# Fp32 hybrid decoder block: the third memory head's keys ahead of the fourth's, the first head's division two units later

## The chip, the cores and the metric

The kernel runs on one core of a Trainium2 chip. The core has five engines, each with its own instruction queue: TensorE (PE in the profile, with its weight loads as PEld), VectorE (DVE), ScalarE (ACT), GpSimd (POOL) and SyncE (SP), which here issues most transfers. Engines wait for each other through semaphores; each works through its own queue in order. The metric is the device time of one execution, in microseconds (us); the time of a kernel is the median of several executions.

## The reference

One decoder layer over 1024 tokens of width 1024, in float32. The parts that the change touches are the keys and values of the memory attention, and the forgetting attention.

```python
u = rms_norm(h, norm_mix[l])
proj = u @ w_in[l]
u_ssm, q, k, v, f_logit, gate_logits = jnp.split(proj, [...], axis=-1)
y_ssm = jax.nn.gelu(s5_ssm(u_ssm, ...))
att = forgetting_attention(q, k, v, f_logit + b_forget[l])   # 8 heads of width 64, causal
h = h + (gate_a * out_a + gate_b * out_b) @ w_mix_out[l]
h = h + memory_cross_attention(rms_norm(h, norm_mem_q[l]), rms_norm(mem, norm_mem_kv[l]), ...)
h = h + (jax.nn.silu(f_a) * f_b) @ w_ffn_out[l]
return rms_norm(h, norm_final)

# forgetting_attention, for one block of queries
s = einsum('bhqd,bhkd->bhqk', qb, kh) * scale + cb[..., :, None] - cum[..., None, :]
p = softmax(where(causal, s, -inf))
out = einsum('bhqk,bhkd->bhqd', p, vh)

# memory_cross_attention: 256 memory tokens, 4 heads of width 128
k, v = split(m @ w_kv, 2, axis=-1)
```

## The kernel before

Each float32 operand is held as a high part (a cast to fp32r on ACT, line 183) and a low part (the rest, a subtraction on DVE, line 184); the helper is `split`. A product is then three matmuls: high by high, low by high, high by low (lines 173 to 175).

The **input stage** (`stage_in`) does four things at once. It loads the two memory tiles and the eight token tiles, computes their norms (squares on ACT, roots on DVE and POOL, the scaling on line 231), transposes them on TensorE (line 237, in PSUM banks named `misc`, `pv` and `mm`) and splits the result into `mh`/`ml` (memory) or `uh`/`ul` (tokens). It splits the weights of the memory's keys and values and of the state-space input into `whi`/`wlo`. It computes the keys of four memory heads (`keys`, 8 steps of three 128x256 matmuls each, in `mm` banks), their values (sums named `sc`), and the first products of the state-space branch (`mm<-uh,whi`). What is written when is told by the string `ORDER_IN`, one word for each step: `K2` is the product for the third head's keys, `k2` its split, `W2` the split of its weight, `T20` and `T21` the transposes of token tile 2, `E20` and `E21` their split (`Em0`, `Em1`, `En0`, `En1` for the two memory tiles), `V` a quarter of the values, `U00` the first state-space product.

The order of this string is not yet the order on the engines. The framework's scheduler places the instructions: each engine takes first what by the scheduler's own estimates of durations is ready first, and the written order decides between them; `behind` adds an edge by hand. So a step that is moved in the string moves others with it.

The **forgetting attention** (`Fox.run`) goes through eight heads. For each it has 12 units: unit `i` computes the scores of one block of 128 keys against up to 512 queries (`scores`, lines 1793 and 1794 in banks `sc`), the exponential on ACT (line 1800), a high and a low part (`ph`, `pl`; in some units the cast is on DVE, line 1802, and the subtraction on POOL, line 1803), and the products with the values two units later (lines 1818 to 1825 in banks `pv`). Work of other heads is laid beside the units: the projection of the head after next (lines 173 to 175 into `mm`, read by ACT and DVE on lines 1725 to 1733), and the running maximum of the next head (`row_max`: line 1763 on TensorE into `mm`, lines 1765 and 1768 on DVE). There are three `mm` banks; projections hold them for long.

When a head is done, its sums `num` are copied out (line 1827), the denominators go through DRAM and come back as `rb`, and `divide` multiplies `num` by `rb` (line 1846), splits the result into `ahi` and `alo` (lines 183 and 184) and stores both. It is called in the next head, behind unit 5. There is one buffer for `num`, so the next head's copy on line 1827 waits until `alo` has been made.

Of the kernel before, what the change touches and what calls it, by code (L numbers as in the profile page):

```python
# [38 lines left out]
RSLOT_LATE = (0, 1, 2, 3, 4, 4, 5, 5, 6, 6, 7, 7)  # L39

ORDER_IN = """
Fm G0 Fn G1 D0 X10 B0 b0 Qm Qn Rm D1 Sm F1 B1 Tm0 Tm1 b1 Rn Sn Tn0 F0 D2 Em0 Tn1 En0 W0 Em1 En1 D3 F2 F3 W1 C1 Q0 Q1 K0 D4 F4 F5 K1 R0
S0 T00 T01 k0 E00 Q2 W2 D5 F6 F7 E01 S1 T10 Q3 W3 k1 K3 K2 W4 E10 W5 D6 R1 k2 T11 k3 S2 Q4 V0 S3 T30
E11 D7 D8 D9 Da Q5 T20 R2 T21 E21 E20 S4 E30 W6 Db y0 L0 W7 T40 V1 S5 E40 T31 V2 E31 W8 T41 V3 E41 W9 T50 Q6 v T51 E51
U00 Q7 R3 S6g u00 L1 T60 E50 S7g Wa T61 T70 E61 Wb U10 E60 T71 E70 E71 P0 y1 U20 u10 u20 P1 U21 U11 U30
P2 u30 U31 u11 u31 U01 u21 P3 P4 P5 u01
# [1531 lines left out]
class Fox:  # L1578
# [280 lines left out]
    def run(self, y_d, yT, aT, w_glu, w_d, filler):  # L1859
# [8 lines left out]
        def load_y(k, h):  # L1868

            with B.behind(self.maxima[NH - 2] if h else self.spread[NH - 4]):  # L1870
                for i, dst in enumerate(yT.rhs(k, h)):
                    S.dma_start(f32(dst).rearrange("p (t c) -> p t c", t=4),
                                y_d[k, i, 4 * h:4 * h + 4].rearrange("t p c -> p t c"))

        def first_glu(i, f):
            with B.behind(self.spread[3] if i < 9 else self.maxima[NH - 2]):
                f()

        def load_att(k):
            for h in range(2):  # L1880
                for i, dst in enumerate(aT.rhs(k, h)):
                    S.dma_start(f32(dst), self.att_d[i, k * P:(k + 1) * P, 512 * h:512 * h + 512])
# [31 lines left out]
        for h in range(NH):  # L1914
            side = {i: [] for i in range(12)}
            late = h == NH - 2
            if late:
                for i, f in enumerate(pro[h + 1].parts[8:]):
                    side[i // 2].append(f)
                side[3].append(pro[h + 1].evac[1])  # L1920
            if h + 1 < NH:
                for i, f in enumerate(self.row_max(h + 1)):
                    side[(RSLOT_LATE if late else RSLOT)[i]].append(f)
                side[9].append(lambda: self.max_row(h + 1))
            if h + 2 < NH:
                n = 8 if h + 3 == NH else 16
                for i, f in enumerate(pro[h + 2].parts[:n]):
                    side[i if n == 8 else PSLOT[i]].append(f)
                side[9].append(pro[h + 2].evac[0])
                if n == 16:  # L1930
                    side[11].append(pro[h + 2].evac[1])
            if h + 3 < NH:
                side[9].append(lambda: pro[h + 3].split(self.exp))
            for n_ in {1: (4, 5), 2: (6,), 3: (7,)}.get(h, ()):
                side[5].append(lambda n_=n_: pro[n_].load(self.spread[h - 1]))
            if h == 0:
                side[0].append(lambda: self.values_of_v(0, 7))
            if late:
                for k in range(8):
                    side[4 + k].append(lambda k=k: load_y(k % 4, k // 4))  # L1940
            if h == NH - 1:
                for k in range(3):
                    side[6 + k].append(lambda k=k: load_att(k))
                for i, f in enumerate(filler):
                    side[i * 12 // len(filler)].append(lambda i=i, f=f: first_glu(i, f))
            for i, u in enumerate(units):
                self.scores(h, *u)
                for f in side[i]:
                    f()
                if len(self.hi_todo) > 2:  # L1950
                    self.values_hi()
                if len(self.lo_todo) > 1:
                    self.values_lo()
                if h and i == 5:
                    with B.behind(self.left):
                        self.divide(h - 1)
        while self.hi_todo:
# [33 lines left out]
```

## Time and profile before

| | us |
|---|---|
| median of 3 runs | 1540.33 (1538.91 to 1540.62) |
| the profiled execution | 1539.77 |
| its span, first to last instruction | 1538.1 |

The profile is of one execution. Its timeline gives for each instruction the start and the duration in us, the engine, the line, what it writes and reads, and in brackets the idle time of the engine before it with what ended it. Matmuls are pipelined: on TensorE the distance between two starts, not the duration, is what one costs.

### The profile page before, as it was taken

What the parts mean: (1) busy time and instruction counts of PE and PEld (TensorE: products, weight loads), DVE (VectorE), ACT (ScalarE), POOL (GpSimd) and SP (SyncE); (2) the same over time, 40 slices, a digit from 0 to 9 for tenths busy, and PEclk for the clock granted to TensorE, in tenths of its full rate; (3) what the DMA queues carried; (4) which work ended last, traced back from release to release, by engine and by line L of the source; (5) the groups of instructions that cost most, each with busy time, mean ns of one, the idle gap of its engine ahead of it and who ended that gap; (6) DMA issues with size and microseconds to landing.
All of it is one profiled execution on the core that took longest, in us unless ns stands there. A gap on an engine that the chain in (4) does not pass through costs nothing. (4 is left out here: it accounts for less than half of the span.)

```text
span 1538.1 us, 20434 instructions
## 1 busy us (share of the span) xinstructions
PE 1520.7 (99%) x7329; PEld 1257.7 (82%) x7329; DVE 1005.7 (65%) x1828; ACT 658.1 (43%) x1183; POOL 253.6 (16%) x341
## 2 busy tenths in 40 slices
PE   8999999999999999999999999999999999999998
PEld 7888888898777678888888888888888888888886
DVE  7936554355878867675556797777777775675555
ACT  7423334324667643232435663333333333354343
POOL 1166542100121214100102200000000000101001
PEclk9999999999999999999999999999999999999999
DMA  9634556611223746378210356555544544896542
GB/s 286 161 104 102 131 128 144 180 41 16 50 46 88 192 131 198 111 218 308 89 69 1 117 204 210 162 161 160 158 158 157 157 145 139 291 391 220 192 163 110
DMA packets 196293, 234.06 MB, mean 152 GB/s; under 512 B 35576, under 2 KB 127656, under 8 KB 195680
## 3 DMA queue, kind: packets, MB, share of 16 engines
q1 hardware_dynamic: 188704, 214.93, 47.0%
q10 hardware_dynamic: 7488, 17.83, 3.1%
q8 instruction: 57, 0.93, 0.3%
q14 instruction: 44, 0.36, 0.1%
HBM read 161.94 MB, written 72.71 MB: 153 GB/s over the span
## 5 line engine op out<-in xcount | busy, mean ns | idle before, releaser
L184 DVE TENSOR_TENSOR wlo<-raw,whi 128x1024 fp32r<-128x1024 f32 (+2 forms) x120 | 126.3, 1058 | 45.4 <-ACT whi L183 44.2
L183 ACT CAST whi<-raw 128x1024 fp32r<-128x1024 f32 (+2 forms) x120 | 108.7, 910 | 105.6 <-PE mm L174 39.1
L184 DVE TENSOR_TENSOR ol<-or,oh 128x1024 fp32r<-128x1024 f32 x73 | 90.1, 1236 | 74.0 <-ACT oh L183 71.9
L173 PE MATMUL mm<-uh,whi 128*128 128x512 f32 x344 | 136.5, 397 | 0.0
L174 PE MATMUL mm<-ul,whi 128*128 128x512 f32 x344 | 135.1, 393 | 0.0
L175 PE MATMUL mm<-uh,wlo 128*128 128x512 f32 x344 | 134.5, 391 | 0.0
L183 ACT CAST oh<-or 128x1024 fp32r<-128x1024 f32 x73 | 76.9, 1054 | 105.0 <-PE mm L1108 34.2
L997 POOL TENSOR_TENSOR g<-a,c 128x512 f32<-128x512 f32 x22 | 35.7, 1621 | 389.0 <-ACT a L996 389.0
L175 PEld LDWEIGHTS mm<-uh,wlo 128*128 128x128 f32 x344 | 64.7, 188 | 13.3 <-DVE wlo L184 0.2
L1803 POOL TENSOR_TENSOR pl<-pf,ph 128x512 fp32r<-128x512 f32 (+1 forms) x32 | 36.8, 1152 | 232.5 <-DVE ph L1802 193.3
L173 PEld LDWEIGHTS mm<-uh,whi 128*128 128x128 f32 x344 | 64.8, 188 | 11.6
L174 PEld LDWEIGHTS mm<-ul,whi 128*128 128x128 f32 x344 | 64.8, 188 | 11.0
L1800 ACT ACTIVATE pf<-sc 128x512 f32<-128x512 f32 (+1 forms) x96 | 46.4, 489 | 44.5 <-DVE sc L1796 28.3
L986 DVE SCALAR_TENSOR_TENSOR c<-c,pv 128x512 f32<-128x512 f32 x22 | 15.1, 687 | 76.5 <-ACT c L985 76.4
L211 POOL TENSOR_TENSOR r<-ms,mhalf 128x1 f32<-128x1 f32 (+1 forms) x26 | 15.7, 605 | 298.6 <-DVE ms L207 258.5
L964 PE MATMUL pv<-S3h,we 128*128 128x512 f32 x176 | 57.7, 389 | 0.0
L1806 DVE TENSOR_TENSOR pl<-pf,ph 128x512 fp32r<-128x512 f32 (+2 forms) x64 | 35.3, 553 | 10.4 <-ACT ph L1805 9.8
L1108 PE MATMUL mm<-ol,oh 128*128 128x512 f32 (+1 forms) x110 | 41.9, 381 | 0.0
L1108 PE MATMUL mm<-oh,ol 128*128 128x512 f32 (+1 forms) x110 | 41.9, 381 | 0.0
L1108 PE MATMUL mm<-oh 128*128 128x512 f32 (+1 forms) x110 | 41.9, 381 | 0.0
L173 PE MATMUL sc<-uh,whi 128*128 128x512 f32 x104 | 40.8, 392 | 0.0
L173 PE MATMUL mm<-yh,whi 128*128 128x512 f32 x104 | 40.7, 392 | 0.0
(639 smaller groups left out, 4554.2 us busy)
## 6 DMA issues: line engine op xcount, KB each, us to landing
or<-c_d SPq DMA_DIRECT2D x77, 256.0 KB
wo<-in_w_ffn_out_dram SPq DMA_DIRECT2D x22, 512.0 KB
c_d<-g SPq DMA_DIRECT2D x44, 256.0 KB
t_d<-wo SPq DMA_DIRECT2D x44, 256.0 KB
or<-t_d SPq DMA_DIRECT2D x44, 256.0 KB
rawb<-in_w_ffn_in_dram SPq DMA_DIRECT2D x20, 512.0 KB
raw<-in_w_ffn_in_dram SPq DMA_DIRECT2D x20, 512.0 KB
raw<-in_w_in_dram SPq DMA_DIRECT2D x19, 512.0 KB
```

The source lines that it names most:

```text
L173: T.matmul(ps, lh, rh, start=first, stop=False)
L174: T.matmul(ps, lh, rl, start=False, stop=False)
L175: return T.matmul(ps, ll, rh, start=False, stop=last)
L183: cast = self.A.copy(hi, src)
L184: self.rest = (self.G if pool_lo else self.V).tensor_sub(lo, src, f32(hi))
L211: self.G.tensor_tensor(out=r, in0=v, in1=self.mhalf[:, 0:n], op=ALU.pow)
L964: T.matmul(ps, l_[:, k, :], r_, start=first and k == 0 and i == 0, stop=k == 3 and i == 2, skip_group_check=True)
L997: G.tensor_mul(g[:, 512:], a1, c1)
L1108: T.matmul(ps, l_[:, gi], r_[:, c0:c1], start=k == 0 and (p == NP - LAST if own else p == 0 and n in (1, 2, 7)), stop=p == NP - 1 and k == ...
L1800: self.exp = A.activation(pf[:, off:], ps[:, off:], AF.Exp)
L1803: G.tensor_sub(pl[:, off:], pf[:, off:], f32(ph[:, off:]))
L1806: self.left = V.tensor_sub(pl[:, off:], pf[:, off:], f32(ph[:, off:]))
```

## The change

In `ORDER_IN` the step `Em1` (the second half of a memory tile's cast and subtraction) is written ahead of the transposes `Tn1`, and `K2` ahead of `K3`. In the attention, `divide` is called behind unit 7 in the second head (`h == 1`, so for the first head's sums) and behind unit 5 in the others, as before. Nothing is added or taken away.

```diff
-Fm G0 Fn G1 D0 X10 B0 b0 Qm Qn Rm D1 Sm F1 B1 Tm0 Tm1 b1 Rn Sn Tn0 F0 D2 Em0 Tn1 En0 W0 Em1 En1 D3 F2 F3 W1 C1 Q0 Q1 K0 D4 F4 F5 K1 R0
-S0 T00 T01 k0 E00 Q2 W2 D5 F6 F7 E01 S1 T10 Q3 W3 k1 K3 K2 W4 E10 W5 D6 R1 k2 T11 k3 S2 Q4 V0 S3 T30
+Fm G0 Fn G1 D0 X10 B0 b0 Qm Qn Rm D1 Sm F1 B1 Tm0 Tm1 b1 Rn Sn Tn0 F0 D2 Em0 Em1 Tn1 En0 W0 En1 D3 F2 F3 W1 C1 Q0 Q1 K0 D4 F4 F5 K1 R0
+S0 T00 T01 k0 E00 Q2 W2 D5 F6 F7 E01 S1 T10 Q3 W3 k1 K2 K3 W4 E10 W5 D6 R1 k2 T11 k3 S2 Q4 V0 S3 T30
...
-                if h and i == 5:
+                if h and i == (7 if h == 1 else 5):
                     with B.behind(self.left):
                         self.divide(h - 1)
```

What the scheduler makes of it is seen at three places. The first is the input stage. On TensorE, behind the second head's products, there stood before (`whi_328` and `wlo_329` are the third head's weight, `whi_349` and `wlo_350` the fourth's, `mm_355` here the fourth head's sum, `xt_205` the first token tile):

```order
L175 MATMUL mm_272<-mh1_0_111,wlo_233 128x256
L173 MATMUL mm_355<-mh0_0_110,whi_349 128x256
L174 MATMUL mm_355<-ml0_0_112,whi_349 128x256
L237 MATMUL misc_306<-ident_69,xt_205 128x128 x4
L237 MATMUL pv_311<-ident_69,xt_205 128x128 x4
L173 MATMUL mm_380<-mh0_0_110,whi_328 128x256
```

Now 11 products of the third head (whose sum is now `mm_355`) stand ahead of the transposes; the last of them, the transposes, and what follows:

```order
L175 MATMUL mm_355<-mh0_0_110,wlo_329 128x256
L173 MATMUL mm_355<-mh0_0_110,whi_328 128x256
L174 MATMUL mm_355<-ml0_0_112,whi_328 128x256
L237 MATMUL misc_306<-ident_69,xt_205 128x128 x4
L237 MATMUL pv_311<-ident_69,xt_205 128x128 x4
L175 MATMUL mm_355<-mh0_0_110,wlo_329 128x256
L173 MATMUL mm_355<-mh1_0_111,whi_328 128x256
```

The fourth head's 24 products now stand in one piece behind the third's. At the end of the same stage, on DVE, ahead of the first state-space product (weight `whi_577`, `wlo_578`; its last token tile comes from `misc_472`), before:

```order
L184 TENSOR_TENSOR ul0_0_95<-misc_472,uh0_0_87 128x2x128
L209 TENSOR_SCALAR ms2_652<-ss2_611 128x2
L184 TENSOR_TENSOR ul3_0_101<-pv_556,uh3_0_93 128x2x128
L215 TENSOR_TENSOR rt2_654<-r02_653 128x2
L216 SCALAR_TENSOR_TENSOR rt2_654<-rt2_654,ms2_652 128x2
L217 SCALAR_TENSOR_TENSOR r02_653<-rt2_654,r02_653 128x2
L184 TENSOR_TENSOR wlo_578<-xw_465,whi_577 128x1024
L184 TENSOR_TENSOR ul1_0_97<-misc_472,uh1_0_89 128x2x128
L184 TENSOR_TENSOR kv_319<-sc_439,kv_318 128x512
L184 TENSOR_TENSOR kv_319<-sc_446,kv_318 128x512
```

And now:

```order
L209 TENSOR_SCALAR ms2_652<-ss2_611 128x2
L184 TENSOR_TENSOR kv_319<-sc_439,kv_318 128x512
L184 TENSOR_TENSOR ul3_0_101<-pv_556,uh3_0_93 128x2x128
L215 TENSOR_TENSOR rt2_654<-r02_653 128x2
L216 SCALAR_TENSOR_TENSOR rt2_654<-rt2_654,ms2_652 128x2
L184 TENSOR_TENSOR wlo_578<-xw_465,whi_577 128x1024
L184 TENSOR_TENSOR ul0_0_95<-misc_472,uh0_0_87 128x2x128
L184 TENSOR_TENSOR kv_319<-sc_446,kv_318 128x512
L184 TENSOR_TENSOR ul1_0_97<-misc_472,uh1_0_89 128x2x128
```

The token tile's low part `ul0_0_95` now stands behind the weight's, and one of the value sums (`sc_439`) ahead of both; on ACT the casts moved likewise. On TensorE the transposes into `misc_472` now stand eight products later, and the next four transposes stand behind the sixth state-space product instead of the first.

The second place is the second head, on DVE, around the division:

```order
 L1802 CAST ph<-pf 128x512
+L1768 TENSOR_REDUCE mc<-mm 128x1
+L1727 SCALAR_TENSOR_TENSOR hb_3274<-mm,hb_3273 64x512
+L1806 TENSOR_TENSOR pl<-pf,ph 128x512
+L1765 ISA junk,mc<-mm,tri 128x384
+L1765 ISA mc 128x1
 L1846 TENSOR_TENSOR num<-num,rb 64x1024
-L1768 TENSOR_REDUCE mc<-mm 128x1
-L1727 SCALAR_TENSOR_TENSOR hb_3274<-mm,hb_3273 64x512
+L1796 TENSOR_TENSOR sc<-sc,trk 128x128
```

The reduction of line 1768, a part of the projection and the next maximum (line 1765) now stand ahead of the division on line 1846.

The third place is the start of the third head, on TensorE (`mm<-hb_3271,hb_3273` are the fourth head's products for its running maximum, `sc<-hb` the third head's first scores):

```order
 L174 MATMUL mm<-ul_0_97,whi 128x512
+L1763 MATMUL mm<-hb_3271,hb_3273 128x128
 L175 MATMUL mm<-uh_0_89,wlo 128x512
+L1825 MATMUL pv<-pl,vhi 65x128
+L1763 MATMUL mm<-hb_3271,hb_3273 128x256
+L1763 MATMUL mm<-hb_3271,hb_3273 128x384
+L173 MATMUL mm<-uh_0_91,whi 128x512
+L174 MATMUL mm<-ul_0_99,whi 128x512
+L1763 MATMUL mm<-hb_3271,hb_3273 128x512
 L1793 MATMUL sc<-hb 128x512
 L1794 MATMUL sc<-hb 128x512
```

The maximum's products, which stood between the scores, now stand ahead of them. At the fourth head's start it is the other way round: there the scores have moved ahead.

## The prediction

> **What bounds the kernel now.** I read the page first, then the waits of TensorE, then the busy time by stretch, then the timelines around the two edits.
>
> ```profile
> span 1538.1 us, 20434 instructions
> PE 1520.7 (99%) x7329; PEld 1257.7 (82%) x7329; DVE 1005.7 (65%) x1828; ACT 658.1 (43%) x1183; POOL 253.6 (16%) x341
> ```
>
> TensorE (PE) is busy for 1520.7 of 1538.1 us, so what an edit can win from idle time is at most the 17.4 us between the two. The list of waits says where such idle time is; its columns are total us, times, longest.
>
> ```profile
> PE sc L258 <- POOL ident masks.py:199: 1.9, 1, 1.9
> PE mm L1763 <- DVE mc L1768: 1.2, 1, 1.2
> PE mm L173 <- ACT whi L183: 1.1, 1, 1.1
> ```
>
> The first is the wait for the identity matrix at the very start. The change lies at the other two: the last is the memory heads' place in the input stage, the middle one the first division of the attention. The stretches (us, then busy PE, PEld, DVE, ACT, POOL, granted clock, DMA) say what stands around them.
>
> ```profile
> 20.00:40.00 20.00, 18.65 (x121) 16.11 (x121) 19.25 (x38) 15.51 (x33) 1.70 (x3) 1.00 0.93 236
> 40.00:60.00 20.00, 19.98 (x106) 16.04 (x105) 16.47 (x49) 13.27 (x27) 5.47 (x3) 1.00 0.81 186
> 400.00:440.00 40.00, 38.73 (x188) 29.57 (x188) 32.59 (x79) 24.81 (x47) 7.92 (x7) 1.00 0.43 79
> ```
>
> From 20 to 40 us VectorE (DVE) is busy for 19.25 of 20, more than TensorE. So a lead won by TensorE there meets, a little later, data that DVE and ScalarE (ACT) make no earlier. In the attention DVE is at 32.6 of 40: loaded, not full. The clock is 1.00 throughout and plays no part.
>
> **The change, part one: the third head's key products ahead of the fourth's.** The second head's last products, the wait, and what follows:
>
> ```profile
> 17.83 0.28 PE L173 MATMUL mm<-mh,whi 128*128 128x256 f32 x1
> 20.19 0.28 PE L175 MATMUL mm<-mh,wlo 128*128 128x256 f32 x1
> 21.58 0.39 PE L173 MATMUL mm<-mh,whi 128*128 128x256 f32 x1 [1.11 <-ACT whi L183]
> 22.32 0.66 PE L237 MATMUL misc<-ident,xt 128*128 128x128 f32 x4 [0.23 <-DVE xt L231]
> 17.16 1.07 ACT L183 CAST whi<-raw 128x1024 fp32r<-128x1024 f32 x1
> 20.46 1.07 ACT L183 CAST whi<-raw 128x1024 fp32r<-128x1024 f32 x1
> 20.98 2.48 DVE L231 SCALAR_TENSOR_TENSOR xt<-xt,r,gain 128x1024 f32<-128x1024 f32 x2
> ```
>
> Of the second head's 24 products the 4th starts at 17.83 and the 24th at 20.19: 0.118 us each. The next could start at 20.31; it starts at 21.58, because it reads the fourth head's high part, cast at 20.46. The third head's part was cast at 17.16. So 1.27 us are lost. After the change 11 products of the third head fit in, 20.31 to 21.60. Then come the transposes of a token tile, and these need its scaling on DVE: two of 1.24 us from 20.98, so the first is there at 22.22. **The removed wait is therefore followed by one of 0.7 us**, and the transposes stay at 22.32. TensorE then has 11 of the two heads' 48 products behind it, not 2: a lead of 9 x 0.118 = **1.06 us**. No DMA is added.
>
> The step `Em1`, moved beside it, changes one thing: on DVE the memory tile's subtraction now stands ahead of the first weight's.
>
> ```profile
> 14.00 1.22 DVE L184 TENSOR_TENSOR wlo<-raw,whi 128x1024 fp32r<-128x1024 f32 x1
> 17.61 0.39 PE L175 MATMUL mm<-mh,wlo 128*128 128x256 f32 x1 [0.16 <-DVE wlo L184]
> ```
>
> The first weight's low part may come some 0.3 us later by that. But DVE's work in sum is the same, and the second head's first low product at 17.61 already waits for its own weight's low part, the last of these subtractions. So a delay of the first head is hidden by that wait; if it isn't, 0.3 are lost. I take nothing.
>
> How long does the lead last? The next rows are those of the first state-space product, at the stage's end.
>
> ```profile
> 43.51 0.47 PE L173 MATMUL mm<-uh,whi 128*128 128x512 f32 x1
> 43.99 0.63 PE L237 MATMUL misc<-ident,xt 128*128 128x128 f32 x4
> 44.38 0.48 PE L174 MATMUL mm<-ul,whi 128*128 128x512 f32 x1
> 40.75 1.05 ACT L183 CAST whi<-xw 128x1024 fp32r<-128x1024 f32 x1
> 41.70 0.38 ACT L183 CAST uh<-misc 128x256 fp32r<-128x256 f32 x1
> 41.96 0.60 ACT L183 CAST kv<-sc 128x512 fp32r<-128x512 f32 x1
> 42.29 1.22 DVE L184 TENSOR_TENSOR wlo<-xw,whi 128x1024 fp32r<-128x1024 f32 x1
> 43.43 0.42 DVE L184 TENSOR_TENSOR ul<-misc,uh 128x256 fp32r<-128x256 f32 x1
> ```
>
> With the lead the first state-space product is reached at 43.51 - 1.06 = 42.45. Its second product reads the low part of the last token tile. In the new order that subtraction stands on DVE behind the weight's (42.29 before), which needs the weight's cast on ACT (40.75 before), which now stands behind the cast of the first value sums. Those sums are complete some 7 products and two groups of transposes ahead of 42.45, so at about 40.4; the cast takes 0.5 to the next issue (41.96 to 42.44 before), a token cast 0.26 (41.70 to 41.96), the weight's cast 1.05: 42.25. The weight's subtraction occupies DVE for 1.14 (42.29 to 43.43), so until 43.4, the token's 0.4: 43.85. So the second product starts at 43.85, having stood ready since 42.7. Before, it starts at 44.38, but with four transposes ahead of it (43.99, some 0.4 us to the next start) that now come later. **Of 1.06 us some 0.1 is left.** From 40 us on PE is busy for 19.98 of 20, so this rest is carried on. Bounds: nothing kept, and all of 1.06 kept. I take 0.1, nearest to the DVE row.
>
> **Part two: the first head's division two units later.**
>
> ```profile
> 404.63 0.40 PE L1763 MATMUL mm<-hb 68*128 68x512 f32 x1
> 408.80 0.40 PE L1763 MATMUL mm<-hb 68*128 68x512 f32 x1
> 409.74 0.40 PE L1818 MATMUL pv<-ph,vhi 128*65 128x512 f32 x1
> 411.38 0.44 PE L1763 MATMUL mm<-hb 68*128 68x384 f32 x1 [1.24 <-DVE mc L1768]
> 405.07 0.69 DVE L1768 TENSOR_REDUCE mc<-mm 128x1 f32<-128x512 f32 x1 [0.67 <-PE mm L1763]
> 408.69 2.04 DVE L1846 TENSOR_TENSOR num<-num,rb 64x1024 f32<-64x1024 f32 x1 [0.41 <-DMA rb<-rd_d]
> 410.65 0.67 DVE L1768 TENSOR_REDUCE mc<-mm 128x1 f32<-128x512 f32 x1
> 433.78 1.21 DVE L1846 TENSOR_TENSOR num<-num,rb 64x1024 f32<-64x1024 f32 x1
> 408.36 1.29 POOL L1803 TENSOR_TENSOR pl<-pf,ph 128x512 fp32r<-128x512 f32 x1 [2.80 <-DVE ph L1802]
> ```
>
> The score product of the running maximum at 411.38 needs the bank that the reduction at 410.65 reads, and this stands behind the division. Without it the reduction starts once the product of 408.80 is through, 0.44 us later (as from 404.63 to 405.07), ends at 409.92, and TensorE goes on at 409.98: **1.40 us earlier**. The division itself takes 2.04 us where the next head's takes 1.21; it ran beside GpSimd's subtraction of 408.36. In its new place, from about 411.8, GpSimd has nothing, so I take 1.21 (bounds 1.21 and 2.04: the upper one would make all behind it 0.83 later).
>
> The Trainium skill (SBUF — State Buffer, section "SBUF: two separate sides") says that VectorE and GpSimd hold a common port pair by an exclusive lock, so that a VectorE operation with two SBUF inputs is blocked until GpSimd's has ended. By that rule the old division would have ended at 409.65 + 1.21 = 410.86, and the trace has 410.73: they agree to 0.13 us. By the rule the new place costs 1.21; if the 2.04 were the first division's own, all behind it would be 0.83 later, and part two would end 0.5 below nothing.
>
> What is late next? Behind the division come ACT's cast of its result, DVE's remainder, and on ACT the copy of the second head's sums, which waits for the remainder already before:
>
> ```profile
> 410.76 1.05 ACT L183 CAST ahi<-num 64x1024 fp32r<-64x1024 f32 x1 [1.41 <-DVE num L1846]
> 412.07 1.22 DVE L184 TENSOR_TENSOR alo<-num,ahi 64x1024 fp32r<-64x1024 f32 x1
> 413.32 0.58 ACT L1827 COPY num<-pv 65x512 f32<-65x512 f32 x1 [0.24 <-DVE alo L184]
> 423.43 0.58 ACT L1733 CAST hb<-mm 64x512 fp32r<-64x512 f32 x1
> 423.39 0.39 PE L175 MATMUL mm<-uh,wlo 128*128 128x512 f32 x1
> 425.62 0.28 PE L1763 MATMUL mm<-hb,hb 68*128 68x256 f32 x1
> ```
>
> The division now runs from 411.8 to 413.0, the cast to 414.1, the remainder to 415.3, so the copy goes from 413.32 to 415.35: 2.0 us later, where TensorE is 1.4 us earlier. ACT's casts behind it can catch up only from its idle time. I let them catch up nearly all: the last cast of the fourth head's projection (423.43 before, ending at 424.01) then ends at about 423.7. This matters in the new order, where the maximum's products of the fourth head stand at the third head's start, ahead of its scores, and the second of them takes the bank that this cast reads (425.62 before, long after the cast). TensorE gets to it after the product of 423.39 and two short ones (0.3 us), 1.3 us earlier than before: 422.4. **It waits about 1.2 us** there, and of 1.40 us **0.3 is left**. Each us by which the cast comes later costs one. Bounds: all of 1.40 kept, since ACT's idle time might cover everything; below, a cast that catches up nothing, priced among the rivals. No DMA is added; the first head's two stores move with the division on SyncE's queue, ahead of the same load as before.
>
> **The sum**: 1539.77 us for the profiled execution (span and 1.7 around it), less 0.1 and 0.3: 1539.4. The median of the runs is 1540.33, 0.56 above that execution, so 1539.9 as a median.
>
> **Rivals.**
> - *One of the two leads stays.* For it: PE is 99.9% busy from 40 to 60 us, and ACT only at 24.8 of 40 in the attention. Against: DVE at 19.25 of 20, and the new bank wait. It gives 1540.33 - 1.4 = 1538.9.
> - *Both stay*: 1540.33 - 1.06 - 1.40 = 1537.9. It needs both bank and weight to come earlier than their chains of rows allow.
> - *Slower: the late remainder holds ACT.* For it: the copy already waited for it; against: ACT's idle time. If all 2.0 us of the copy's delay reach the cast that ended at 424.01, the bank comes at 426.0 instead of 423.7, and the 0.3 left of part two become 2.0 lost: with part one's 0.1 some 1542.2. It decides from a cast that ends past 424.0.
> - *It does not do what it says*: the scheduler does place the products and the division as asked, but at the cast and the reduction TensorE may lose the same time to the next wait, whole: 1540.3.
>
> **How the numbers follow.** The forecast of 1539.9 (own range 1539.2 to 1540.6) has 0.40, one lead 0.27, both 0.15, slower 0.08, no gain at all 0.10. The range from 1537.6 to 1541.8 leaves out 0.15 and takes in the bounds of both parts. A measurement of this kernel can tell about 0.2% from no change, 3.1 us; only both leads and somewhat more (0.05), or the slower rival at more than its price (0.03), get there, so 0.92 lies within.
>
> **What would show it.** Right: no wait of 1.1 us for the cast near 20.3, but one of 0.7 for the scaling near 21.6, and a wait of about 1 us for DVE near 43; no wait of 1.2 for the reduction near 410, a division of 1.2 us near 412, and a wait of about 1 us for ACT at the third head's start. Wrong: TensorE passes 43 or 423 without waiting (then the leads stay), or the third head's wait is over 2 us.

## The result, and the profile after

| | us |
|---|---|
| before, median of 20 runs | 1540.30 |
| after, median of 20 runs | 1543.51 |
| ratio | 1.0021 (95% interval 1.0015 to 1.0027) |
| forecast | 1539.9, range 1537.6 to 1541.8 |

The change makes the kernel 3.2 us slower; the forecast was 0.4 us faster, with a range that ends at 1541.8. One of the 20 runs of after was slow (2245.35 us at a granted clock of 0.632), and the ratio leaves it out. The profiled execution of after took 1543.80 us, 4.0 more than the one of before. First the page's span and busy times of after, then its list of TensorE's waits (total us, times, longest):

```profile
span 1542.1 us, 20435 instructions
PE 1522.5 (99%) x7329; PEld 1257.7 (82%) x7329; DVE 1005.7 (65%) x1828; ACT 658.3 (43%) x1183; POOL 255.7 (17%) x341
```

```profile
PE sc L1793 <- ACT pf L1800: 1.3, 3, 0.6
PE mm L1763 <- ACT hb L1733: 1.0, 2, 0.8
PE mm L1763 <- DVE mc L1768: 0.9, 1, 0.9
PE mm L174 <- DVE ul L184: 0.8, 1, 0.8
PE mm L175 <- DVE wlo L184: 0.8, 1, 0.8
```

The wait of 1.1 us for the fourth head's weight (line 173 on `whi`) is gone, and the stall of 1.2 us in the second head is gone too, though a reduction of line 1768 is listed again: it stands in another head. Waits of 0.6 to 0.9 us have come in their place, of five kinds (the first stood at 0.7 us before). Where they lie shows when the same instruction of the program is looked up in both timelines (start, duration). Before:

```profile
62.49 0.39 PE L173 MATMUL mm<-uh,whi 128*128 128x512 f32 x1
407.31 0.39 PE L174 MATMUL mm<-ul,whi 128*128 128x512 f32 x1
412.12 0.40 PE L1793 MATMUL sc<-hb,hb 69*128 69x512 f32 x1
453.37 0.40 PE L1794 MATMUL sc<-hb,hb 128*128 128x512 f32 x1
1513.78 0.39 PE L1108 MATMUL mm<-ol,oh 128*128 128x512 f32 x1
```

The same five after:

```profile
64.16 0.39 PE L173 MATMUL mm<-uh,whi 128*128 128x512 f32 x1
408.94 0.39 PE L174 MATMUL mm<-ul,whi 128*128 128x512 f32 x1
412.36 0.40 PE L1793 MATMUL sc<-hb,hb 69*128 69x512 f32 x1
457.23 0.39 PE L1794 MATMUL sc<-hb,hb 128*128 128x512 f32 x1
1517.80 0.39 PE L1108 MATMUL mm<-ol,oh 128*128 128x512 f32 x1
```

TensorE is 1.67 us late behind the input stage and carries that unchanged to the second head of the attention (1.63). There the removed stall brings it back to 0.24: 1.39 us, where 1.40 was forecast. By the fourth head it is 3.86 late, so 3.6 us were lost between 412 and 457. Behind that it is 4.0 late to the end.

**The input stage after.** The lead's start, and what the stage does with it:

```profile
22.45 0.66 PE L237 MATMUL misc<-ident,xt 128*128 128x128 f32 x4 [0.61 <-DVE xt L231]
44.38 0.50 PE L174 MATMUL mm<-ul,whi 128*128 128x512 f32 x1 [0.81 <-DVE ul L184]
52.48 0.50 PE L175 MATMUL mm<-uh,wlo 128*128 128x512 f32 x1 [0.78 <-DVE wlo L184]
42.76 1.23 DVE L184 TENSOR_TENSOR wlo<-xw,whi 128x1024 fp32r<-128x1024 f32 x1
45.17 0.15 DVE L217 SCALAR_TENSOR_TENSOR r<-rt,r 128x2 f32<-128x2 f32 x1
45.35 1.15 ACT L228 ACTIVATE xt<-xt,r 128x1024 f32<-128x1024 f32 x1 [0.62 <-DVE r L217]
46.58 4.76 POOL L229 TENSOR_TENSOR xt<-xt,gain 128x1024 f32<-128x1024 f32 x2 [4.72 <-DMA kv_d<-kv]
50.26 2.17 DVE L184 TENSOR_TENSOR wlo<-xw,whi 128x1024 fp32r<-128x1024 f32 x1 [0.53 <-ACT whi L183]
```

The wait at 44.38 is the forecast's. The one at 52.48 is not: it is for the second state-space weight's low part, whose subtraction took 2.17 us, where the first weight's took 1.23. GpSimd (POOL) was scaling the last two token tiles from 46.58 to 51.34. Before, it did that 2.9 us earlier, and was through when VectorE came:

```profile
42.21 0.16 DVE L217 SCALAR_TENSOR_TENSOR r<-rt,r 128x2 f32<-128x2 f32 x1
43.69 4.78 POOL L229 TENSOR_TENSOR xt<-xt,gain 128x1024 f32<-128x1024 f32 x2 [1.91 <-ACT xt L228]
48.44 1.23 DVE L184 TENSOR_TENSOR wlo<-xw,whi 128x1024 fp32r<-128x1024 f32 x1 [0.53 <-ACT whi L183]
```

GpSimd waits for ScalarE's scaling (line 228), and that for the last step of the token roots (line 217), which the new order puts behind the first weight's subtraction: 45.17 instead of 42.21. (In after the bracket of GpSimd's row names a store of the values, which this operation does not read; ScalarE's row ends at 46.50, 0.08 us ahead of it, and in `k_only` the same row names line 228.)

What the second wait costs shows at four transposes that have 24 of the state-space products ahead of them in every one of these kernels. They start at 50.18 before, at 50.65 here and at 49.91 in the input part alone (`in_only`, below). Seven products later TensorE stands at 52.01, 53.51 and 52.78. So the wait costs 1.0 us between two starts in both kernels, while the 0.74 us between these two, whose order in this stage is the same, were there ahead of it.

**The attention after**, from the second head to the start of the fourth:

```profile
410.87 0.69 DVE L1768 TENSOR_REDUCE mc<-mm 128x1 f32<-128x512 f32 x1 [0.96 <-PE mm L1763]
411.62 0.44 PE L1763 MATMUL mm<-hb 68*128 68x384 f32 x1
413.39 1.21 DVE L1846 TENSOR_TENSOR num<-num,rb 64x1024 f32<-64x1024 f32 x1
416.97 0.58 ACT L1827 COPY num<-pv 65x512 f32<-65x512 f32 x1 [0.42 <-DVE alo L184]
424.37 0.58 ACT L1733 CAST hb<-mm 64x512 fp32r<-64x512 f32 x1
425.00 0.56 PE L1763 MATMUL mm<-hb,hb 68*128 68x256 f32 x2 [0.81 <-ACT hb L1733]
436.47 1.29 POOL L1803 TENSOR_TENSOR pl<-pf,ph 128x512 fp32r<-128x512 f32 x1 [2.76 <-DVE ph L1802]
436.82 2.01 DVE L184 TENSOR_TENSOR alo<-num,ahi 64x1024 fp32r<-64x1024 f32 x1 [0.44 <-ACT ahi L183]
438.76 0.67 DVE L1768 TENSOR_REDUCE mc<-mm 128x1 f32<-128x512 f32 x1
439.49 0.44 PE L1763 MATMUL mm<-hb,hb 68*128 68x384 f32 x1 [0.94 <-DVE mc L1768]
452.39 0.39 PE L1793 MATMUL sc<-hb,hb 69*128 69x256 f32 x1 [0.58 <-ACT pf L1800]
454.92 0.50 PE L1763 MATMUL mm<-hb 68*128 68x512 f32 x1 [0.21 <-DVE mc L1765]
```

At 410.87 the reduction no longer waits for the division, and TensorE goes on. At 425.00 stands the forecast's wait for the bank. At 436.82 the picture of the old stall comes back one head later: the remainder `alo` of the second head's sums stands ahead of the reduction on VectorE, takes 2.01 us beside GpSimd's subtraction of 436.47, and TensorE waits 0.94 for the reduction behind it. Two more waits follow at the fourth head's start. The four brackets make 2.5 us; by the distance between starts, over what the same places take without a wait (0.23 us for a product of 512 columns), they are some 1.0, 1.1, 0.5 and 0.4 us, 3.0 of the 3.6.

### The profile page after: what moved, and what is told of

The parts are those of the page before. It is cut to its first block, busy times and chain, and to the rows that moved or that the text cites. A ratio compares the mean times of both kernels' runs of the same rounds, so it can differ in the third digit from the quotient of the medians.

```text
span 1542.1 us, 20435 instructions
## 1 busy us (share of the span) xinstructions
PE 1522.5 (99%) x7329; PEld 1257.7 (82%) x7329; DVE 1005.7 (65%) x1828; ACT 658.3 (43%) x1183; POOL 255.7 (17%) x341
```

## The experiments

Each kernel was timed in 11 runs against the kernel before on the same chip (27 to 33 runs, medians 1539.93, 1540.16 and 1540.03 in the three groups). A ratio is worked out from all runs and is not quite that of the two medians; what is called shown goes by its interval.

### The parts alone

**The input part alone** (`in_only`): the division is behind unit 5 again.

```diff
-                if h and i == (7 if h == 1 else 5):
+                if h and i == 5:
```

> The input stage's part alone; the division stays behind unit 5. Theory (the loss of the changed kernel is the sum of two losses that do not touch each other, 1.7 us in the input stage and some 2.3 in the attention by the two profiles): about 1.7 us slower than before, some 1542.0, with the wait of about 0.9 us for the second state-space weight's low part at about 52.5, and the stall of 1.2 us for the reduction near 412 as before. Rival (the input stage kept what was forecast, 0.1 us gained, and the rest is how one execution fell): 1540.2.

Measured 1540.82 us, ratio 1.0001 (0.9993 to 1.0010). Both waits are there (0.81 at 43.64 and 0.76 at 51.74, with a subtraction of 2.17), and behind the stage TensorE is 0.9 us late. But the expected stall in the second head was not there in this execution: see `div_6` below. By the interval the input part lies between 1.1 us faster and 1.5 us slower, so a loss is not shown by the time.

**The division's part alone** (`div_only`): `ORDER_IN` as before.

> The division's part alone; the input stage is that of before. Theory (separate losses): the stall of 1.24 us for the reduction in the second head is gone, and in the third and fourth heads some 3.5 us come back (waits of about 0.8 us for the bank at the third head's start, 0.9 for the reduction behind the remainder in the third head, and about 0.5 each at two places of the fourth head's start): 1.5 to 2.3 us slower than before, some 1542.2. Rival (the division keeps 0.3 us, as forecast): 1540.0.

Measured 1543.08, ratio 1.0020 (1.0011 to 1.0029). So by the medians nearly the whole loss is here, 3.1 us, more than the 1.5 to 2.3 expected (the interval goes from 1.7 to 4.5). The waits at the third and fourth heads are those of after. The profiled execution has one wait more, of 1.43 us at 542.05 in the seventh head, where a division waits 1.73 us for its transfer (0.45 before); one other kernel shows such a wait (`div_max`, 0.93 us at 539.87), after does not, and how often it comes and what makes it was not studied.

**The two halves of the input part.** `em_only` moves only the cast `Em1`, `k_only` only puts `K2` ahead of `K3`.

```diff
-... Em0 Tn1 En0 W0 Em1 En1 ...
+... Em0 Em1 Tn1 En0 W0 En1 ...
```

> Only the step of the memory tile's cast written earlier; TensorE's and ScalarE's orders are those of before, and on VectorE one subtraction of the memory tile changes places with the first weight's. Theory (as forecast, the second head's own wait hides it): no change, 1540.2, with a wait of 0.2 to 0.3 us near 15.9 for the first weight's low part, and the second head's wait near 17.6 gone. Rival (it is not hidden): 0.3 us slower, 1540.5.

Measured 1540.15, ratio 0.9999 (0.9990 to 1.0008): nothing, with a wait of 0.27 us for the first weight's low part at 15.61 and none at the second head, as expected.

> Only the third head's key products written ahead of the fourth's, without the earlier cast. Theory (this alone makes the input part's loss): the waits of 0.8 us near 44 and 0.8 near 52 of the input part, and its time, 1540.8. Rival (the earlier cast is what sets the later order): no waits there, 1539.2.

Measured 1541.07, ratio 1.0009 (1.0000 to 1.0018). Both waits are there, 0.81 us at 44.28 and 0.76 at 52.38, the second behind the same long subtraction:

```profile
50.16 2.17 DVE L184 TENSOR_TENSOR wlo<-xw,whi 128x1024 fp32r<-128x1024 f32 x1 [0.52 <-ACT whi L183]
```

So the two heads' key products that change places make the input part's waits, without the earlier cast.

### Is it the meeting with GpSimd?

**GpSimd made to wait** (`in_gain`): the input part, and GpSimd reads one column of the second weight's low part before it scales the last tile (the rest of the edit hands `w` and `mark` through). No other engine's order changes.

```diff
...
-            self.G.tensor_mul(xs, xs, gb)
+            with self.behind(self.G.tensor_copy(self.mark, f32(w[:, 0, 0:1])) if w is not None else None): self.G.tensor_mul(xs, xs, gb)
...
```

> The input stage's part alone, and GpSimd copies one column of the second state-space weight's low part (128x1) before it scales the last token tile, so that this scaling starts only when VectorE's subtraction for that weight is done; the order on the other engines is the same. Theory (VectorE's subtraction took 2.17 us because GpSimd's scaling ran beside it): the subtraction takes 1.2 us again, TensorE's wait near 52.5 falls from 0.9 to under 0.1, and the kernel is 0.9 us faster than the input part alone, some 1541.1. Rival (the weight is late because its cast on ScalarE and the rows ahead of it on VectorE are late): the subtraction still ends at about 52.4, and the time is that of the input part alone, 1542.0; if the later scaling delays the last tile's transposes, slower than that.

Measured 1543.07, ratio 1.0018 (1.0009 to 1.0027): the theory had the time wrong, the rival the subtraction, and the trace says why.

```profile
50.58 1.22 DVE L184 TENSOR_TENSOR wlo<-xw,whi 128x1024 fp32r<-128x1024 f32 x1 [0.52 <-ACT whi L183]
52.01 2.38 POOL L229 TENSOR_TENSOR xt<-xt,gain 128x1024 f32<-128x1024 f32 x1
52.17 2.30 DVE L1304 COPY prow<-ldr 16x128 f32<-16x128 f32 x1
55.89 0.23 PE L1307 MATMUL misc<-ident,prow 48*128 48x48 f32 x1 [1.92 <-issue]
```

With GpSimd held off, the subtraction takes 1.22 us and TensorE's wait for it is gone: that much of the theory is shown. But the scaling now meets the next VectorE operation that works from SBUF to SBUF, a copy of 16x128 that takes 0.22 us alone. It is held until the scaling ends and takes 2.30, and TensorE is idle for 1.92 us ahead of the transpose of its result. The profile names no releaser there. The copy ends at 54.47 and the transpose starts at 55.89; in between VectorE catches up with two subtractions that empty `misc` banks, the second from 55.36 to 55.78, so the bank may be what came last. The collision was not removed but moved to a worse place.

The idle time is not the whole loss. Here is TensorE from 57 to 61 us, first in this kernel and then in `in_only` (length, busy time with the number of products, granted clock, DMA share, GB/s):

```profile
57.00:61.00 4.00, 4.00 (x13) 0.57 0.96 175
57.00:61.00 4.00, 4.00 (x23) 1.00 1.00 184
```

Behind the gap the granted clock is 0.57, and products start 0.43 us apart (57.84, 58.27, 58.70) instead of 0.23. At 0.57 for 4 us some 1.7 us more are lost, which is an estimate from these rows. None of the other kernels' traces shows a lower clock there. That the gap brings the lower clock on is not shown by one trace.

**The order at the stage's end mended** (`in_wv`): the input part, with the value sums' split (`v`) written behind `S6g` and, by an edge, behind the first state-space weight's cast.

```diff
-... T50 Q6 v T51 E51
-U00 Q7 R3 S6g u00 ...
+... T50 Q6 T51 E51
+U00 Q7 R3 S6g v u00 ...
...
-            B.split(kv[2][:, cs], kv[3][:, cs], ps.pop(("v", t)))
+            with B.behind(first_w): B.split(kv[2][:, cs], kv[3][:, cs], ps.pop(("v", t)))
```

> The input stage's part alone, with the split of the value sums written later and put behind the first state-space weight's cast: on ScalarE this cast is again ahead of the value cast, and on VectorE the last step of the token roots is again ahead of that weight's subtraction, so that GpSimd scales the last two token tiles earlier. Theory (the lead of the key products is lost at two places: behind the first weight's late cast, and where the second weight's subtraction meets GpSimd's scaling): GpSimd is through before the subtraction starts, this takes 1.2 us, not 2.2, TensorE's wait near 52 is gone, the wait near 44 is under 0.5 us, and the kernel is 1.3 us faster than the input part alone, some 0.4 faster than before: 1539.5. Rival (the lead is lost earlier in the stage): the time of the input part alone, 1540.8.

Measured 1539.50, ratio 0.9996 (0.9988 to 1.0005). That interval overlaps the one of `in_only`, so the time alone does not show the 1.3 us. The rows are as the theory has them: GpSimd starts at 43.64, the subtraction is short, and only the first wait is left.

```profile
43.64 4.75 POOL L229 TENSOR_TENSOR xt<-xt,gain 128x1024 f32<-128x1024 f32 x2 [2.05 <-ACT xt L228]
43.91 0.50 PE L174 MATMUL mm<-ul,whi 128*128 128x512 f32 x1 [0.58 <-DVE ul L184]
49.45 1.23 DVE L184 TENSOR_TENSOR wlo<-xw,whi 128x1024 fp32r<-128x1024 f32 x1 [0.53 <-ACT whi L183]
```

The four transposes that started at 50.18 before start at 50.20 here. So with the second wait gone nothing is lost, but the lead is spent all the same.

### Is it the late division, or the order of the heads behind it?

**The division behind unit 8** (`div_8`), one unit later still. On every engine the third and fourth heads then stand as before the change.

```diff
-                if h and i == 5:
+                if h and i == (8 if h == 1 else 5):
```

> The division of the first head one unit later still (behind unit 8 instead of 7), the input stage as before; on all engines the third and fourth heads then stand in the order of before, while the reduction stands ahead of the division as in the change. Theory (it is the new order of the third and fourth heads that costs, not the late division): the stall of 1.24 us goes, nothing comes back in the third and fourth heads, and the kernel is about 1.0 us faster than before, some 1539.3. Rival (the late remainder delays ScalarE's copy and casts, and so the banks, whatever the order): no gain or a loss, 1540.3 to 1542.

Measured 1539.48, ratio 1.0000 (0.9991 to 1.0008). Its interval ends below the start of that of `div_only`: a later division alone costs nothing, so the loss needs the order of the heads behind it. (No run has that order with an early division.) ScalarE's copy on line 1827 comes at 416.31, 3.0 us later than before, and still the last cast of the fourth head's projection runs at 422.24, ahead of the 423.43 before. The gain of 1.0 is not shown: 0.4 by the medians, nothing by the ratio. In the trace the stall is gone, and 0.5 us of it are lost again at the second head's end.

**The maximum held back** (`div_max`): the division behind unit 7, and the fourth head's products for its maximum behind the third head's scores.

```diff
-            with B.behind((self.parted, self.scored)[h] if h < 2 else None):
+            with B.behind(self.parted if h == 0 else self.scored if h in (1, 3) else None):
```

> The division's part alone, with the fourth head's products for its maximum held behind the scores written ahead of them, so that the third head's start has the scores first again. The remainder stays ahead of the reduction on VectorE in the third head. Theory (the losses of the third head are two of about 1.1 us each, the bank at its start and the remainder ahead of the reduction, and the start of the fourth head adds some 1.2): the first goes, the kernel takes 1.0 us less than the division's part alone, 1542.0. Rival (the bank wait only hides another one, since ScalarE is late in any order): no change, 1543.1.

Measured 1540.78, ratio 1.0004 (0.9996 to 1.0013): 2.3 us less than `div_only`, where 1.0 was expected. The wait of 0.82 us at the third head's start is gone, those of the fourth head's start are gone with it, and the remainder meets GpSimd for a shorter time:

```profile
435.21 1.28 POOL L1803 TENSOR_TENSOR pl<-pf,ph 128x512 fp32r<-128x512 f32 x1 [2.10 <-DVE ph L1802]
435.91 1.67 DVE L184 TENSOR_TENSOR alo<-num,ahi 64x1024 fp32r<-64x1024 f32 x1 [0.43 <-ACT ahi L183]
438.23 0.44 PE L1763 MATMUL mm<-hb,hb 68*128 68x384 f32 x1 [0.36 <-DVE mc L1768]
```

The remainder still stands ahead of the reduction, but takes 1.67 us, not 2.01, and TensorE waits 0.36, not 0.94. But the edge has moved more than the third head's start: in the trace TensorE's fourth head also begins in the order of before again. So the run shows that a division behind unit 7 costs little without these two orders (its interval ends at 1.0013), and not whether the early maximum set the fourth head's waits off or that head's own order made them.

### The kernel before once more

**The division behind unit 6** (`div_6`): the order on every engine is that of before.

> The first head's division one unit later (behind unit 6), the rest as before: by the scheduler the order on every engine is then the order of before, so this is the kernel before once more. Theory (whether the division or GpSimd's subtraction takes 2 us is decided from execution to execution, by whether the denominators' transfer lands before or after GpSimd starts, some 3.6 us behind the transfer's issue): the same time as before, within 0.05%, and in the profile either a division of 2.0 us or more with a stall of TensorE of 1.2, or one of 1.2 us beside a GpSimd subtraction of 2.4 with a stall under 0.4. Rival (the short division seen with the input part alone came from that part): 2.0 us and the stall of 1.2.

Measured 1540.38, ratio 1.0001 (0.9993 to 1.0010). The division, GpSimd's subtraction and the product that stalled before:

```profile
408.57 1.22 DVE L1846 TENSOR_TENSOR num<-num,rb 64x1024 f32<-64x1024 f32 x1
408.73 2.22 POOL L1803 TENSOR_TENSOR pl<-pf,ph 128x512 fp32r<-128x512 f32 x1 [2.80 <-DVE ph L1802]
410.44 0.44 PE L1763 MATMUL mm<-hb 68*128 68x384 f32 x1
```

With the same order on every engine the division now takes 1.22 us, GpSimd's subtraction 2.22, and no stall is listed. Seven kernels were profiled with the division behind unit 5 in order. In five (before, `em_only`, `k_only`, `in_gain`, `in_wv`) the denominators' transfer landed after GpSimd had started: the division took 1.80 to 2.29 us, the stall 1.24. In two it landed ahead (`in_only`, `div_6`): 1.22 us, no stall listed, and GpSimd was held instead. `in_only` shows how close it is: both start at 409.38, 3.62 us behind the transfer's issue.

```profile
405.76 0.50 SPq L1840 DMA_DIRECT2D rb<-rd_d  x1
409.38 1.22 DVE L1846 TENSOR_TENSOR num<-num,rb 64x1024 f32<-64x1024 f32 x1
409.38 2.36 POOL L1803 TENSOR_TENSOR pl<-pf,ph 128x512 fp32r<-128x512 f32 x1 [2.80 <-DVE ph L1802]
```

### The mended parts together

**Both gains** (`both_fixed`): `in_wv` with the division behind unit 8.

> The input part with the later value split, and the first head's division behind unit 8. Theory (the parts do not touch each other): the two gains add up, 0.4 from the one and 0.4 from the other: 0.8 us faster than before, 1539.1. Rival (what is won is lost further on): 1539.9.

Measured 1540.00, ratio 0.9997 (0.9988 to 1.0006). A gain over either part is not shown.

**The change, mended** (`mended`): both parts as they are, with the edges of `in_wv` and `div_max`.

> The whole change (both parts, the division behind unit 7) with two additions: the later split of the value sums in the input stage, and the fourth head's maximum behind the third head's scores. Theory (the give-backs are these orders and no others, and the parts add up): the division with the maximum held back was 0.6 us slower than before, the input part with the later split 0.6 faster: some 1540.2, 3.3 us faster than the change. Rival (something else of the change costs): over 1541.5.

Measured 1540.10, ratio 0.9998 (0.9990 to 1.0007), 3.4 us less than after. The two additions take away all of the loss; they do not make the change a gain. No kernel of this study beats the one before by more than its interval.

One more thing differs from profile to profile. In five of the thirteen (`em_only`, `div_max`, `in_gain`, `both_fixed`, `mended`) TensorE waits 0.50 to 1.01 us near 27.5 to 28 for the subtraction that makes a token tile's low part, whichever order the keys have; in before and after it does not. What makes it was not studied, and a difference of that size between two single profiles is not yet one of their kernels.

## Why the prediction failed, step by step

- **What bounds the kernel** held: TensorE is at 99% in both, with the same 7329 products. By the page its idle time went from 17.4 to 19.6 us; the rest of the 4.0 us is counted as busy.
- **The removed wait of part one** held in mechanism. The transposes came at 22.45 (22.32 was forecast).
- **The first state-space product** came out near the forecast: 43.85 was forecast, and its second product started at 44.38 in after, 44.28 in `k_only` and 43.64 in `in_only`. The wait ahead of it was 0.81 in all three. So the half microsecond in after is one execution's: the value product that started at 42.45 before started at 41.86 there, a lead of 0.59, and at 41.12 in `in_only`, a lead of 1.33.
- **"So this rest is carried on" failed.** The step took TensorE's 19.98 busy of 20 from the profile of before as a promise that nothing behind the first product comes late. In the new order something does: the last step of the token roots had moved behind the weight's subtraction (the rows of VectorE's order ahead of the prediction begin to differ there, and the step no longer stands in them), and by ScalarE and GpSimd this reaches the second weight 5 us later. The term of 0.1 us won became 1.0 us lost at that wait, and TensorE was 1.67 us late behind the stage in after, 0.9 in `in_only`. `in_wv` shows the mechanism: with that step back in its place the subtraction takes 1.23 us and the wait at 52 is gone.
- **The moved cast at nothing** held: `em_only`.
- **The removed stall of part two** held: 1.39 us in the profiled execution. But by the seven profiles the stall is there in five executions of seven, so what its removal is worth on average is less than one profile says.
- **The division at 1.21** held. The rule of the Trainium skill (SBUF — State Buffer, section "SBUF: two separate sides"), that VectorE and GpSimd hold a common port pair by an exclusive lock, agrees with the rows shown here within 0.2 us, and with which of the two starts first. It was applied only to the place that the division left. The two places where the new order makes such a meeting, 50.26 and 436.82, are what the sum lacked.
- **The late copy and the bank** held to a few tenths: the copy was to be 2.0 us late, and is (416.97 less 413.32, less the 1.63 by which TensorE came late). The last cast was to end at 423.7; it ends at 424.95, which is 423.3 less the same 1.63. The bank wait was to be 1.2 and is 0.81.
- **"Of 1.40 us 0.3 is left" failed.** The sum ended at the third head's start. Behind it the new order had the remainder ahead of the reduction in the third head, and another order at the fourth head's start: 0.94, 0.58 and 0.21 us of waits, some 2.1 us by the distance between starts, which the sum had at nothing. `div_8`, without these orders, does not have the loss, and `div_max`, which keeps only the remainder ahead of the reduction, has little of it.
- **The slower rival** had the sign but not the mechanism. It put the loss on the copy's delay; `div_8` divides later still, has the copy 3.0 us later, and loses nothing.
- **The parts**: 0.9 and 3.1 us by the medians, against 3.2 together, which their intervals allow. The interval of `in_only` holds zero, so of the input part only the mechanism is shown, not its size in the time.

## What to carry to other kernels

A moved step in a scheduled program is priced along every row that the order changes, to the last one, not only to the first wait that follows it: here the losses lay 8 us behind the last place that was looked at in the input stage, and 14 to 30 us behind it in the attention. Where two engines can hold each other up, look for new meetings at every place that moves, as well as for the old one that goes. A stall that a single profile shows may be one outcome of a race with a transfer; what its removal is worth needs several executions.

## What the runs showed of the hardware

- The hold works both ways, and the one that is held ends about its own time after the other's end: GpSimd's 128x512 subtraction takes 1.29 us alone, 2.36 when the division starts at the same time and 2.22 when the division starts 0.16 us ahead; the division takes 1.21 alone and 1.80 to 2.29 behind it.
- In these rows it is the place of the operands that counts, not the size: a copy of 16x128 from SBUF to SBUF was held for 2.30 us, while in after the subtractions of line 184 that read a PSUM bank ran in 0.42 us beside the same scaling:

```profile
46.80 0.42 DVE L184 TENSOR_TENSOR ul<-misc,uh 128x256 fp32r<-128x256 f32 x1 [1.48 <-ACT uh L183]
```

- Which engine is held can change between executions with the same order on every engine (before and `div_6`), and a stall of TensorE of 1.2 us comes or goes with it.
